# A two-layer streaming trunk on one core: norm matmuls, one branch tile, layer-B norms, value tiles and key weights reordered

## The chip, the core and the metric

The kernel runs on one core of a Trainium2 chip. The core has a matrix engine (TensorE, "PE"; its weight loads are listed as "PEld"), a vector engine (DVE), an activation engine (ACT), a general engine (POOL) and a queue engine (SP) which here only issues DMA transfers. ACT and POOL issue transfers too. Each engine works through its own stream in order; semaphores tie the streams together. Matmul results go to PSUM, which the kernel uses as eight banks of 128 x 512 float32, and ACT or DVE bring them to SBUF.

The metric is device time of one execution in microseconds, the median of several runs. Lower is better.

## The reference, cut to what matters

One inference step over 1024 prompt frames and 32 sample frames (1056 columns), model width 1024. Layer A is a gated linear recurrence, layer B is banded attention, and both read the residual stream through RMS norms:

```python
# layer A (width 1408, 16 blocks of 88 for the gates)
u = rmsnorm(x, norm_pre) @ w_in                 # branch | gate
conv = conv_b + sum(ext[:, tap:tap+T] * conv_w[tap] for tap in range(4))
r = sigmoid(conv_blocks @ w_r + b_r); i = sigmoid(conv_blocks @ w_i + b_i)
a = exp(-8 * r * softplus(-lam)); b = sqrt(1 - a*a) * (i * conv)
h = scan(a, b)                                  # h_t = a_t h_(t-1) + b_t
x1 = x + rmsnorm((h * silu(gate)) @ w_out, norm_post)
# shared keys and values
kv = rmsnorm(x1, norm_kv) @ w_kv;  k = rope(kv[:256]);  v = kv[256:]
# layer B: 16 query heads on 4 key heads, window 128, a sink per head
u = rmsnorm(x1, norm_pre_b) @ w_in_b;  q = rope(u[:1024])
y = x1 + rmsnorm((attend(q, k, v) * silu(u[1024:])) @ w_out_b, norm_post_b)
```

Outputs are `y` for all frames, the last convolution inputs and recurrence states, the keys and values of the last 128 prompt frames and those of the sample frames.

## The kernel before, in words

**Tiles.** Activations are held transposed: 128 channels on the partitions, frames along the free axis. The frames fall into three column blocks, n = 0, 1, 2, of 384, 384 and 292 columns in layer A (`NSA`; 292 with gaps) and 384, 384 and 288 in layer B (`NSB`). Weights come as 128 x 128 tiles.

**Three matmuls for one.** Each float32 operand is split into a high part (rounded) and a low part (the rest). A product is three matmuls: high by high, high by low, low by high (`mm3`, lines 150 to 152, and `mm3_steps`, line 698, which yields after every six matmuls so that others can be put between). The high part is made on ACT (line 116, or 120 with a gain), the low part on DVE (line 117 or 121), for a few weights on POOL.

**Weights.** `weights` loads a matrix in groups of four 128 x 128 tiles into a ring called `raw` (four buffers, shared by every weight of the kernel) and splits them into rings `whi` and `wlo` (six buffers each). A gain of a norm is folded in: for the names in `GAIN_ACT` in the split itself, for others by a product on POOL first (line 132).

**The order.** Each engine's stream is laid out when the kernel is built, by a planner which simulates the engines and takes, among the instructions that it thinks ready, the one that comes first in the program. `urgent()` moves an instruction ahead by 300 places. `pin()` ties an instruction behind the one which the program names before it on the same engine. At run time the streams are fixed: an engine whose next instruction isn't ready waits.

**The start of layer A.** The three first branch tiles are multiplied column block by column block (`first_mm`, with x not yet normed), because x arrives in blocks. `x_stat(n)` makes the row statistics and a diagonal matrix of the norm's scale; `x_norm(n)` spreads it over the partitions with one matmul per 128 frames (line 296, tile `rs`), then scales the open PSUM banks (line 207, DVE), and runs the convolution (line 222 on ACT, 224 on DVE) and the split of its result into `chi` and `clo`. `x_norm(0)` comes behind branch tile 1 of block 1, `x_norm(1)` behind branch tile 0 of block 2, `x_norm(2)` at the end.

**The loop over the other branch tiles** (line 445): step t multiplies branch tile t (t from 3), loads weights two tiles ahead, and runs the gate matmuls of tile t - 3 (`GATES_AT`). Gate blocks of 88 channels don't agree with tiles of 128, so a gate takes its own tile (three matmuls, lines 150 to 152, tile `gt`) and a few rows of the neighbours, which `pack_rows` copies by DMA into a tile `pack` (line 371, matmuls at 390 and 391). The first gates stand in step 3, behind branch tile 3.

**From layer A to layer B.** The w_out_a product runs block by block, eight output tiles each (`oa`). Beside it the norms run as generators: `norms_a(n)` has eleven steps, namely the residual loads (16 transfers for block 2), the post-norm's sum (`ss_p`, line 158) and factor, one step for each of eight tiles (scale on DVE, line 601; add the residual, 607; split into `xh`, `xl`; square), and at last the second norm's sum (`ss_x`) and factor `r1`, which scales the rope tables on POOL (636). `NORM_AT` says how many steps of which block's generator run behind each output tile, `NORM_KV` how many in each key block: its first entry inside `rope`, behind the key matmuls, its second behind the value rows.

**Keys and values.** For each column block: `k_block(n)` multiplies the two key halves (`rAk`, `rBk`, 24 matmuls each, line 698), runs `norm()`, rotates (715 to 717), splits and stores; then `v_rows(n)` makes two value tiles (`vc`, lines 150 to 152), scaled by `r1` (765). `v_blocks(n)` transposes them, 128 frames at a time (`v_block(t)`, two pinned transposes, line 775), and splits and stores the result. The blocks of n = 0 and 1 are transposed behind the next key block, all three at once; those of n = 2 behind the first query block, when PSUM has been divided anew and matmul tiles have three banks.

**Layer B** goes on with query blocks (`q_block`, the same `rope`), attention head group by head group with gate tiles and the next group's queries between, and the output product with its norm. The last 256 frames leave through `out_t`.

Of the kernel before, what the change touches and what calls it, by code (L numbers as in the profile page):

```python
# [9 lines left out]
F32 = mybir.dt.float32  # L10
# [7 lines left out]
P = 128  # L18
# [45 lines left out]
def _trunk(ctx, tc, nc, A):  # L64
# [58 lines left out]
    def weights(src, kn, name, gain=None):  # L123

        out = []
        for k0 in range(0, kn, 4):
            kk = min(4, kn - k0)
            raw = ring.tile([P, 4, P], F32, tag="raw", bufs=4, name=f"raw_{name}_{k0}")
            nc.sync.dma_start(raw[:, :kk, :], src[:, k0:k0 + kk, :])
            if gain is not None and name not in GAIN_ACT:  # L130
                with urgent():
                    G.tensor_tensor(raw[:, :kk, :], raw[:, :kk, :],
                                    gains[:, gain * KD + k0:gain * KD + k0 + kk].unsqueeze(2).to_broadcast([P, kk, P]),
                                    op=ALU.mult)
            hi = ring.tile([P, 4, P], F32R, tag="whi", bufs=6, name=f"whi_{name}_{k0}")
            lo = ring.tile([P, 4, P], F32R, tag="wlo", bufs=6, name=f"wlo_{name}_{k0}")
            with urgent():
                if name in GAIN_ACT:
                    for i in range(kk):
                        split_scaled(hi[:, i, :], lo[:, i, :], raw[:, i, :], g_of(gain, k0 + i))  # L140
                else:
                    split(hi[:, :kk, :], lo[:, :kk, :], raw[:, :kk, :], G if name in LO_POOL else None, name in HI_DVE)
            out += [(hi[:, i, :], lo[:, i, :]) for i in range(kk)]
        return out

    def mm3(ps, ws, xs, last=True):

        n = len(ws)
        for i, ((wh, wl), (xh, xl)) in enumerate(zip(ws, xs)):
            nc.tensor.matmul(ps, wh, xh, start=i == 0, stop=False)  # L150
            nc.tensor.matmul(ps, wh, xl, start=False, stop=False)  # L151
            nc.tensor.matmul(ps, wl, xh, start=False, stop=last and i == n - 1)  # L152

# [32 lines left out]
    def x_of(c0, c1):  # L186
        return [(xhi[k][:, c0:c1], xlo[k][:, c0:c1]) for k in range(KD)]

    conv, chl, ext, gw, pack = {}, {}, {}, {}, {}

    def branch_mm(t, ns=(0, 1, 2)):
        if t not in ext:
            ext[t] = row(f"ext{t}")
            G.memset(ext[t][:, 0:3], 0.0)
        banks = []
        for n in ns:
            c0, c1 = NSA[n]
            ps = bank(f"br{t}_{n}")
            mm3(ps[:, :c1 - c0], wts[t], x_of(c0, c1))
            banks.append((n, ps))  # L200
        return banks

    def branch_evac(t, banks):
        for n, ps in banks:
            c0, c1 = NSA[n]
            with urgent():
                V.tensor_tensor(ext[t][:, 3 + c0:3 + c1], ps[:, :c1 - c0], rs[:, c0:c1], op=ALU.mult)
# [83 lines left out]
    def x_norm(n):  # L291

        ps = bank(f"rs{n}")
        for i, t in enumerate(range(3 * n, 3 * n + 3)):
            m = P if t < 8 else DEC
            pin(nc.tensor.matmul(ps[:, i * P:i * P + m], ones[:m], diag[:m, t * P:t * P + m], start=True, stop=True))
        with urgent():
            if n < 2:
                S.activation(rs[:, NSA[n][0]:NSA[n][1]], ps[:, :384], AF.Copy, scale=1024.0)
            else:  # L300
                S.activation(rs[:, 768:SEQ], ps[:, :256], AF.Copy, scale=1024.0)
                S.activation(rs[:, S0:S0 + DEC], ps[:, 256:256 + DEC], AF.Copy, scale=1024.0)
        for m in range(NS):
            branch_evac(m, open_[n][m])
        for m in range(NS):
            branch_conv(m, n)

    open_ = {0: [], 1: [], 2: []}

    def first_mm(n, m):  # L310
        if n == 0 and m:
            prep_in(m)
        open_[n].append(branch_mm(m, (n,)))

    x_split(0)
    for m in range(NS):
# [10 lines left out]
    x_stat(1, xr[1])  # L327
    for n in (1, 2):
        for m in range(NS):
            first_mm(n, m)  # L330
            if m == 2 - n:
                x_norm(n - 1)
        if n == 1:
            x_stat(2, xr[2])
    x_norm(2)
# [108 lines left out]
    GATES_AT = ((), (), (), (0,), (1,), (2,), (3,), (4,), (5,), (6,), (7,), (8, 9, 10))  # L444
    for t in range(MR):
        if t >= NS:
            branch_evac(t, branch_mm(t))
        wts.pop(t)
        if t >= NS - 2:
            prep_in(t + 2)  # L450
        with urgent():
            if t >= NS:
                branch_conv(t)
            if t >= 1:
                prep_gate(t - 1)
        ri = [gates(i) for i in GATES_AT[t]]
        with urgent():
            if t >= NS:

                split(*chl[t], conv[t], behind=True)  # L460
            if t >= 1:
                pack_rows(t - 1)
        for i, g in zip(GATES_AT[t], ri):
            recur(i, g)
# [175 lines left out]
            next(na[int(i)], None)  # L640


    NORM_AT = ((), ("0", "00", "00", "00", "00", "", "", ""), ("1", "11", "110", "11", "11", "", "", ""))
    NORM_KV = (("1", "2" * 10), ("", ""), ("2", ""))
    korder = [k for k in range(MR) if k not in LATE] + list(LATE)
    REUSE = 2
    orders = [list(range(KD))]
# [85 lines left out]
    def k_block(n, wA, wB, norm):  # L733
        nm = f"k{n}"
        c0, c1 = NSB[n]
        run(rope(n, wA, wB, nm, norm))
        a, b = rope_out.pop(nm)
        q = halves(nm, a, b, c1 - c0)
        dst = kscr.rearrange("x p c -> p x c")
        if n < 2:  # L740
            nc.sync.dma_start(dst[:, :, c0:c1], q.bitcast(F32))
        else:
            nc.sync.dma_start(dst[:, :, c0:SEQ], q[:, :, :256].bitcast(F32))
            nc.sync.dma_start(dst[:, :, 1152:1184], q[:, :, 256:256 + DEC].bitcast(F32))
            for i, x in enumerate((a, b)):
                nc.sync.dma_start(A["o_k"][i], x[:, 128:256 + DEC])
# [10 lines left out]
    def v_rows(n):  # L757

        c0, c1 = NSB[n]
        out = []  # L760
        for i in range(2):
            ps = bank(f"vc{n}_{i}")[:, :c1 - c0]
            mm3(ps, wts[f"v{i}"], x1_of(c0, c1))
            u = unit(f"vc{n}_{i}", w=c1 - c0)
            V.tensor_tensor(u, ps, r1[:, c0:c1], op=ALU.mult)
            out.append(u)
        return out

    def v_block(t, rows_):
# [11 lines left out]
            nc.sync.dma_start(A["o_v"][(t - 7) * P:(t - 7) * P + m], f[:m, :256])  # L781

    vrows = {}

    def v_blocks(n):
        for t in range(3 * n, 3 * n + 3):
            v_block(t, vrows[n])

    def prep_v():

# [37 lines left out]
    prep_v()  # L828
    for n in range(3):
        k_block(n, wts["kA"], wts["kB"], lambda: pump(NORM_KV[n][0]))  # L830
        if n:
            v_blocks(n - 1)
        vrows[n] = v_rows(n)
        pump(NORM_KV[n][1])
    for nm in ("kA", "kB", "v0", "v1"):
# [138 lines left out]
    def finish_og(g, n):  # L974
# [6 lines left out]
                ogl[m, n] = t  # L981
        del TT[g, n]

    for nm, mi in (("qA0", 0), ("qB0", 1)):
        prep_m(nm, A["w_in_b"][mi], KD, 3)
    for n in range(3):
        run(q_block(0, n))
        if n == 0:
            v_blocks(2)

    def fillers(g):
        for m in (2 * g, 2 * g + 1):
# [253 lines left out]
```

## Time and profile before

| | |
|---|---|
| median of 3 runs | 905.42 us (905.33 to 906.95) |
| profiled execution | 905.81 us, span 904.0 us |
| PE busy | 885.4 us, 98% of the span, 5434 matmuls |
| DVE, ACT, POOL busy | 708.1, 563.1, 221.7 us |
| granted PE clock, mean | 0.995 |
| DMA | 137.35 MB, 152 GB/s |

A row of a timeline gives start, duration, engine, line, operation, output and inputs, and shape; in brackets the idle time ahead of it and what ended it. "x3" merges three such instructions. PE matmuls overlap, so that their durations (0.34 us for 384 columns) are about twice the distance of their starts; the distance is what counts for the time. A row of a stretch gives its bounds, its length, the busy time of each engine with the number of instructions, the granted PE clock as a share, the busy share of the DMA engines and GB/s. A row of the waits gives who waited for whom, the sum, how often, and the longest.

### The profile page before, as it was taken

To read this page: it belongs to the slowest core of one execution; us is meant where nothing else is said; L and a number is where in the kernel's file an instruction comes from. 1 tells how busy PE (TensorE), PEld (TensorE's weight loads), DVE (VectorE), ACT (ScalarE), POOL (GpSimd) and SP (SyncE) were. 2 spreads that over 40 slices of the span, in tenths; PEclk is the share of its full clock that TensorE was granted. 3 is DMA by queue.
4 is the path that set the end of the run, shared out by engine and by line. 5 is a ranking of instruction groups with operands and counts; after the bars stand their busy time and mean duration, and the time that the engine had idled before them with its cause. 6 is when DMAs were issued, how large, how long until landed. Compare 5 with 4: busy or idle time off the path is not lost. (4 is left out here: it accounts for less than half of the span.)

```text
span 904.0 us, 15787 instructions
## 1 busy us (share of the span) xinstructions
PE 885.4 (98%) x5434; PEld 864.4 (96%) x5434; DVE 708.1 (78%) x1499; ACT 563.1 (62%) x1231; POOL 221.7 (25%) x263
## 2 busy tenths in 40 slices
PE   9989999999999999999999999999999999999997
PEld 8989999999999999999989899999999999999975
DVE  6797878878897654177897847999999989998776
ACT  8748877879454325364663527766767757797661
POOL 5250212114300001126362432122122011202330
PEclk9999999999999999999999999999999999999999
DMA  9522433242533216445545667338338338334884
GB/s 337 204 75 77 135 88 125 81 128 92 181 119 124 89 57 190 146 135 178 163 157 186 210 205 205 98 111 231 96 110 239 103 97 239 121 112 160 281 250 144
DMA packets 95777, 137.35 MB, mean 152 GB/s; under 512 B 16144, under 2 KB 64304, under 8 KB 95696
## 3 DMA queue, kind: packets, MB, share of 16 engines
q1 hardware_dynamic: 86040, 123.30, 43.9%
q10 hardware_dynamic: 9480, 12.49, 4.5%
q8 instruction: 43, 0.70, 0.3%
q0 software_dynamic: 176, 0.54, 0.2%
q14 instruction: 38, 0.31, 0.1%
HBM read 99.28 MB, written 32.13 MB: 145 GB/s over the span
## 5 line engine op out<-in xcount | busy, mean ns | idle before, releaser
L150 PE MATMUL oa<-yh,whi_outa 128*128 128x384 f32 (+1 forms) x264 | 85.8, 326 | 0.0
L151 PE MATMUL gb<-xlo,whi_ina 128*128 128x384 f32 (+1 forms) x264 | 85.6, 324 | 0.0
L152 PE MATMUL gb<-xhi,wlo_ina 128*128 128x384 f32 (+1 forms) x264 | 85.4, 323 | 0.0
L150 PE MATMUL gb<-xhi,whi_ina 128*128 128x384 f32 (+1 forms) x264 | 85.2, 323 | 0.0
L151 PE MATMUL oa<-yl,whi_outa 128*128 128x384 f32 (+1 forms) x264 | 85.1, 323 | 0.0
L152 PE MATMUL oa<-yh,wlo_outa 128*128 128x384 f32 (+1 forms) x264 | 85.1, 323 | 0.0
L616 POOL TENSOR_TENSOR qp<-qp,qp 128x384 f32<-128x384 f32 (+2 forms) x34 | 49.3, 1449 | 138.2 <-ACT qp L614 126.5
L150 PE MATMUL br<-xhi,whi_ina 128*128 128x384 f32 (+1 forms) x240 | 77.8, 324 | 0.0
L151 PE MATMUL br<-xlo,whi_ina 128*128 128x384 f32 (+1 forms) x240 | 77.8, 324 | 0.0
L152 PE MATMUL br<-xhi,wlo_ina 128*128 128x384 f32 (+1 forms) x240 | 77.4, 323 | 0.0
L117 DVE TENSOR_TENSOR wlo_outa<-raw_outa,whi_outa 128x512 fp32r<-128x512 f32 (+1 forms) x60 | 43.7, 742 | 42.7 <-ACT whi_outa L116 42.6
L931 ACT ACTIVATE P<-P,sm 128x257 f32<-128x257 f32 (+1 forms) x132 | 64.3, 490 | 8.0 <-DVE sm L928 7.9
L698 PE MATMUL gB<-xl,whi_g 128*128 128x384 f32 (+1 forms) x192 | 63.0, 328 | 0.0
L698 PE MATMUL gB<-xh,whi_g 128*128 128x384 f32 (+1 forms) x192 | 62.9, 328 | 0.0
L698 PE MATMUL gB<-xh,wlo_g 128*128 128x384 f32 (+1 forms) x192 | 62.6, 326 | 0.0
L116 ACT ACTIVATE whi_outa<-raw_outa 128x512 fp32r<-128x512 f32 (+1 forms) x60 | 35.5, 594 | 41.5 <-PE oa L151 25.1
L224 DVE SCALAR_TENSOR_TENSOR conv<-ext,pa,conv 128x1060 f32<-128x1060 f32 (+2 forms) x51 | 50.2, 1005 | 9.0 <-ACT conv L222 8.6
L928 DVE CUSTOM_DVE_ANT_0 P<-S,mask,nsnk 128x256 f32<-128x256 f32 (+1 forms) x128 | 52.8, 463 | 4.9 <-PE S L926 4.8
L151 PEld LDWEIGHTS oa<-yl,whi_outa 128*128 128x128 f32 x264 | 49.6, 188 | 0.4
L150 PEld LDWEIGHTS oa<-yh,whi_outa 128*128 128x128 f32 x264 | 49.6, 188 | 0.4
L150 PEld LDWEIGHTS gb<-xhi,whi_ina 128*128 128x128 f32 x264 | 49.7, 188 | 0.0
L152 PEld LDWEIGHTS oa<-yh,wlo_outa 128*128 128x128 f32 x264 | 49.7, 188 | 0.0
(301 smaller groups left out, 2894.0 us busy)
## 6 DMA issues: line engine op xcount, KB each, us to landing
raw_ina<-w_in_a SPq DMA_DIRECT2D x44, 256.0 KB, 2.8
raw_outa<-w_out_a SPq DMA_DIRECT2D x40, 256.0 KB, 2.7
raw_ob<-w_out_b SPq DMA_DIRECT2D x32, 256.0 KB, 2.6
qscr<-quadq SPq DMA_DIRECT2D x8, 768.0 KB
Q<-qscr SPq DMA_DIRECT2D x32, 192.0 KB, 4.3
hscr<-u SPq DMA_DIRECT2D x11, 530.0 KB, 3.0
xr<-xr SPq DMA_DIRECT2D x8, 512.0 KB, 10.2
raw_g<-w_in_b SPq DMA_DIRECT2D x16, 256.0 KB, 3.3
```

What stands on the lines that cost most here:

```text
L116: pin(S.activation(dst_hi, src, AF.Copy), behind)
L117: (lo_eng or V).tensor_tensor(dst_lo, src, dst_hi.bitcast(F32), op=ALU.subtract)
L150: nc.tensor.matmul(ps, wh, xh, start=i == 0, stop=False)
L151: nc.tensor.matmul(ps, wh, xl, start=False, stop=False)
L152: nc.tensor.matmul(ps, wl, xh, start=False, stop=last and i == n - 1)
L224: V.scalar_tensor_tensor(c, e[:, c0 + k:c1 + k], pa[:, t, k:k + 1], c, op0=ALU.mult, op1=ALU.add)
L616: G.tensor_tensor(sums[0], sums[0], q, op=ALU.add)
L698: nc.tensor.matmul(ps, l, r, start=c == 0, stop=c == 3 * n - 1)
L928: V.tensor_tensor_reduce(pt[:, h, :w], sb[:, (h - h0) * 256:(h - h0) * 256 + w], msk, -0.125, nsnk[:, sk][:, h:h + 1], op0=ALU.add, op1=AL ...
L931: S.activation(pt[:, h, :w + 1], pt[:, h, :w + 1], AF.Exp, bias=nmax[:, h:h + 1], scale=-1.0, accum_out=rsum[:, h:h + 1])
```

## The change

There are seven edits:

1. `mm3` gets a callback `mid`, run in the middle of a product, and a flag `behind` which pins its first matmul. `x_norm(0)` now stands in the middle of branch tile 1 of block 1, and `x_norm(1)` in the middle of branch tile 0 of block 2, with the matmul that follows pinned; the next tile's first matmul is pinned too.
2. Column blocks 0 and 1 of branch tile 4 move into step 3, ahead of the first gates. Column block 2 stays in step 4.
3. The loads of the first key weights (kA) get two buffers of their own in the pool `late` instead of two of the four in the ring.
4. Norm steps: block 1 keeps its eighth tile step for key block 0, and its last step for the place behind the value rows of block 0. Block 2's residual loads and its post-norm's sum move into key block 0, behind the key matmuls; its eight tile steps follow behind the value rows, as before.
5. Value tiles of blocks 0 and 1 are transposed one by one: two inside the next key block (after 18 matmuls of each key half) and one between the two value products.
6. Those of block 2 are spread over the first two query blocks (`V_AT`): after 18 matmuls of the second half of query block 0, and after 18 of each half of query block 1.
7. POOL's gain products of qA1 and qB1 are pinned behind POOL's earlier work in the program.

```diff
+            if name == "kA":
+                raw = late.tile([P, 4, P], F32, tag="raw", bufs=2, name=f"raw_{name}_{k0}")
+            else:
+                raw = ring.tile([P, 4, P], F32, tag="raw", bufs=4, name=f"raw_{name}_{k0}")
...
+                    pin(G.tensor_tensor(raw[:, :kk, :], raw[:, :kk, :],
...
+                                        op=ALU.mult), name in ("qA1", "qB1"))
...
-    def mm3(ps, ws, xs, last=True):
+    def mm3(ps, ws, xs, last=True, mid=None, behind=False):
...
-            nc.tensor.matmul(ps, wh, xh, start=i == 0, stop=False)
+            if mid and i == n // 2:
+                mid()
+            pin(nc.tensor.matmul(ps, wh, xh, start=i == 0, stop=False), behind and i == 0 or mid and i == n // 2)
...
-            first_mm(n, m)
-            if m == 2 - n:
-                x_norm(n - 1)
+            first_mm(n, m, (lambda: x_norm(n - 1)) if m == 2 - n else None, m == 3 - n)
...
-            branch_evac(t, branch_mm(t))
+            branch_evac(t, branch_mm(t, (2,) if t == 4 else (0, 1, 2)))
...
+        if t == 3:
+            branch_evac(4, branch_mm(4, (0, 1)))
...
-    NORM_AT = ((), ("0", "00", "00", "00", "00", "", "", ""), ("1", "11", "110", "11", "11", "", "", ""))
-    NORM_KV = (("1", "2" * 10), ("", ""), ("2", ""))
+    NORM_AT = ((), ("0", "00", "00", "00", "00", "", "", ""), ("1", "11", "110", "1", "1", "1", "", ""))
+    NORM_KV = (("122", "1" + "2" * 8), ("", ""), ("2", ""))
...
-        run(rope(n, wA, wB, nm, norm))
+        for step, _ in enumerate(rope(n, wA, wB, nm, norm)):
+            if n and step in (2, 6):
+                v_block(3 * n - 3 + step // 4, vrows[n - 1])
...
+            if n and i == 0:
+                v_block(3 * n - 1, vrows[n - 1])
...
-        if n:
-            v_blocks(n - 1)
...
+    V_AT = {(0, 6): 6, (1, 2): 7, (1, 6): 8}
...
-        run(q_block(0, n))
-        if n == 0:
-            v_blocks(2)
+        for step, _ in enumerate(q_block(0, n)):
+            if (n, step) in V_AT:
+                v_block(V_AT[n, step], vrows[2])
```

More of the change, by code (lines that the diff above doesn't have):

```diff
@@ L127, in weights @@
             kk = min(4, kn - k0)
-            raw = ring.tile([P, 4, P], F32, tag="raw", bufs=4, name=f"raw_{name}_{k0}")
+            if name == "kA":
+                raw = late.tile([P, 4, P], F32, tag="raw", bufs=2, name=f"raw_{name}_{k0}")
+            else:
+                raw = ring.tile([P, 4, P], F32, tag="raw", bufs=4, name=f"raw_{name}_{k0}")
             nc.sync.dma_start(raw[:, :kk, :], src[:, k0:k0 + kk, :])
@@ L131, in weights @@
                 with urgent():
-                    G.tensor_tensor(raw[:, :kk, :], raw[:, :kk, :],
-                                    gains[:, gain * KD + k0:gain * KD + k0 + kk].unsqueeze(2).to_broadcast([P, kk, P]),
-                                    op=ALU.mult)
+                    pin(G.tensor_tensor(raw[:, :kk, :], raw[:, :kk, :],
+                                        gains[:, gain * KD + k0:gain * KD + k0 + kk].unsqueeze(2).to_broadcast([P, kk, P]),
+                                        op=ALU.mult), name in ("qA1", "qB1"))
             hi = ring.tile([P, 4, P], F32R, tag="whi", bufs=6, name=f"whi_{name}_{k0}")
@@ L189, in _trunk, with branch_mm @@
     conv, chl, ext, gw, pack = {}, {}, {}, {}, {}
-    def branch_mm(t, ns=(0, 1, 2)):
+    def branch_mm(t, ns=(0, 1, 2), mid=None, behind=False):
         if t not in ext:
@@ L198, in branch_mm @@
             ps = bank(f"br{t}_{n}")
-            mm3(ps[:, :c1 - c0], wts[t], x_of(c0, c1))
+            mm3(ps[:, :c1 - c0], wts[t], x_of(c0, c1), mid=mid, behind=behind)
             banks.append((n, ps))
@@ L308, in _trunk, with first_mm @@
     open_ = {0: [], 1: [], 2: []}
-    def first_mm(n, m):
+    def first_mm(n, m, mid=None, behind=False):
         if n == 0 and m:
             prep_in(m)
-        open_[n].append(branch_mm(m, (n,)))
+        open_[n].append(branch_mm(m, (n,), mid, behind))
     x_split(0)
@@ L783, in _trunk @@
     vrows = {}
-    def v_blocks(n):
-        for t in range(3 * n, 3 * n + 3):
-            v_block(t, vrows[n])
     def prep_v():
```

## The prediction

> **What bounds the kernel now.** I read the page, the waits by engine, the busy time of stretches, then the timelines around each hole in TensorE (PE).
>
> ```profile
> span 904.0 us, 15787 instructions
> PE 885.4 (98%) x5434; PEld 864.4 (96%) x5434; DVE 708.1 (78%) x1499; ACT 563.1 (62%) x1231; POOL 221.7 (25%) x263
> ...
> PE gt L150 <- ACT chi L116: 3.6, 1, 3.6
> PE rAk L698 <- DVE xl L117: 1.8, 2, 1.3
> PE rAk L698 <- DVE wlo_kA L121: 1.2, 3, 0.6
> PE v L775 <- DVE rp2q L715: 0.9, 1, 0.9
> ```
>
> PE bounds everything; the change adds and removes no PE work, so only its holes can be won. The four waits lie where the diff works. Their stretches (columns: PE, weight loads, DVE, ACT, POOL busy; granted clock; DMA):
>
> ```profile
> 58.40:62.20 3.80, 0.20 (x3) 0.01 (x1) 3.80 (x8) 1.55 (x4) 1.26 (x1) 0.93 0.02 8
> 62.20:65.50 3.30, 3.30 (x13) 3.30 (x14) 3.21 (x8) 1.28 (x3) 2.53 (x3) 0.56 0.53 148
> 465.60:472.50 6.90, 5.61 (x27) 4.03 (x26) 6.90 (x14) 4.03 (x14) 4.64 (x5) 1.00 0.15 54
> 472.50:504.00 31.50, 31.50 (x181) 30.96 (x180) 24.79 (x57) 14.72 (x40) 10.74 (x11) 1.00 0.63 196
> 504.00:509.80 5.80, 4.02 (x28) 3.55 (x27) 5.80 (x13) 2.07 (x6) 3.75 (x4) 1.00 0.29 108
> 520.50:532.00 11.50, 10.30 (x58) 9.45 (x58) 6.37 (x15) 2.37 (x7) 5.82 (x7) 1.00 0.57 168
> 874.70:877.10 2.40, 0.19 (x2) 0.13 (x2) 0.82 (x3) 2.25 (x5) 1.10 (x1) 1.00 0.93 304
> 877.50:880.90 3.40, 3.40 (x9) 2.49 (x8) 3.30 (x8) 1.27 (x4) 0.00 (x0) 0.50 0.83 228
> ```
>
> ```profile
> 57.38 0.33 PE L150 MATMUL gt<-chi,whi_gate 128*128 128x384 f32 x1
> ...
> 58.26 0.33 PE L152 MATMUL gt<-chi,wlo_gate 128*128 128x384 f32 x1
> 62.19 0.93 PE L150 MATMUL gt<-chi,whi_gate 128*128 128x292 f32 x2 [3.60 <-ACT chi L116]
> ...
> 65.47 0.34 PE L150 MATMUL br<-xhi,whi_ina 128*128 128x384 f32 x1
> ...
> 70.51 0.34 PE L152 MATMUL br<-xhi,wlo_ina 128*128 128x384 f32 x1
> 70.97 0.41 PE L390 MATMUL gt<-pack,whi_gate 96*128 96x384 f32 x1
> ...
> 504.23 0.29 PE L698 MATMUL rAk<-xh,whi_kA 128*128 128x288 f32 x1
> ...
> 506.63 0.29 PE L698 MATMUL rAk<-xh,whi_kA 128*128 128x288 f32 x1
> ```
>
> A 384-column matmul issues every 0.175 us (30 from 65.47 to 70.51), a 288-column one every 0.133 (19 from 504.23 to 506.63). So the gates lose 3.75 us waiting (58.26 + 0.175 to 62.19) and 0.44 x 3.3 = 1.45 to the halved clock, 0.2 more on either side: **5.4**. First key block: 6.9 - 27 x 0.175 = **2.2**. Last key block: 5.8 - 0.175 - 27 x 0.133 = **2.0**. Value tiles 6 to 8: 11.5 - 52 x 0.175 - 6 transposes at about 0.1 = **1.8**. Together 11.4, the most there is to win. (The hole at 874.7 lies in the output stage, which the diff leaves alone.)
>
> **The change part by part.** *Gates and tile 4.* 48 matmuls of tile 4 (8.4 us) now stand before the first gates, so gates start at 57.38 + 8.4 = 65.8, when chi and clo are there:
>
> ```profile
> 25.48 0.68 DVE L289 TENSOR_SCALAR diag<-ident,stat 128x128 f32<-128x128 f32 x3
> ...
> 31.73 1.49 DVE L207 TENSOR_TENSOR ext<-br,rs 128x384 f32<-128x384 f32 x3 [1.82 <-ACT rs L299]
> ...
> 34.74 0.67 DVE L289 TENSOR_SCALAR diag<-ident,stat 128x128 f32<-128x128 f32 x3
> ...
> 62.92 1.19 DVE L117 TENSOR_TENSOR clo<-conv,chi 128x292 fp32r<-128x292 f32 x3
> ...
> 63.07 2.74 ACTq L371 DMA_DIRECT2D pack<-chi  x3
> ...
> 63.39 2.83 SPq L371 DMA_DIRECT2D pack<-clo  x3
> ...
> DMA to landing us min/median/max: 6.5/6.5/6.5
> ...
> 29.64 0.38 PE L296 MATMUL rs<-diag,ones 128*128 128x128 f32 x2
> ...
> 37.70 0.38 PE L296 MATMUL rs<-diag,ones 128*128 128x128 f32 x2
> ```
>
> But what is late next is the packed rows: issued from 63.07 and 63.39, 6.5 us to landing, used at 70.97. Before, 30 matmuls of tile 4 filled that time; now they are spent, and after three native matmuls PE stands before a pack matmul at 65.8 + 0.5 = 66.3: 4.6 us early. The planner placed pack after 18 native and 30 tile-4 matmuls, that is at 57.4 + 2.9 + 5.3 = 65.6 had nothing waited, so it would see no reason to put the remaining 24 matmuls of tile 4 in between. Against this works the earlier norm: block 0's norm matmuls move from behind branch 1 to its middle, 12 x 0.175 = 2.1 us sooner (29.64 to 27.5), block 1's 12 x 0.133 = 1.6 sooner (37.70 to 36.1). The diagonals they read are there at 26.2 and 35.4, so these two pins cost PE nothing. DVE sat idle 1.82 us for rs and is full at 58 to 65 (3.80 of 3.80), so the chain to clo ends some 3 us sooner (2.1 plus scattered idle). Left-over wait 4.6 - 3 = 1.6, no halved clock: **-3.8**. Bounds: -5.4 (pack lands in time); +0.8 (nothing gained by DVE: 4.6 waited, 1.6 at half clock). Tile 4's evacuations, PSUM banks and its row only move; DVE has them to do anyway.
>
> *When the clock halves.* The waits for xl in key block 2 (1.3 us the longer) left the clock at 1.00; the one at 874.7 (2.4 us) was followed by 3.4 us at 0.50. I price a wait of over 2.4 us with 1.6 more. [...]
>
> *Keys and values.*
>
> ```profile
> 459.62 1.40 SPq L129 DMA_DIRECT2D raw_kA<-w_k  x2
> ...
> 490.52 8.41 SPq L580 DMA_DIRECT2D res<-xT  x16
> ...
> 465.68 5.74 DVE L121 SCALAR_TENSOR_TENSOR wlo_kA<-raw_kA,gains,whi_kA 128x128 fp32r<-128x128 f32 x8
> 471.34 2.18 DVE L121 SCALAR_TENSOR_TENSOR wlo_kB<-raw_kB,gains,whi_kB 128x128 fp32r<-128x128 f32 x8
> ...
> 489.94 1.01 DVE L765 TENSOR_TENSOR vc<-vc,r 128x384 f32<-128x384 f32 x2
> ...
> 498.79 0.84 DVE L607 TENSOR_TENSOR z<-z,res 128x288 f32<-128x288 f32 x1 [0.64 <-DMA res<-xT]
> ...
> 511.12 0.54 DVE L765 TENSOR_TENSOR vc<-vc,r 128x384 f32<-128x384 f32 x1
> ...
> 486.57 0.55 PE L698 MATMUL rAk<-xh,whi_kA 128*128 128x384 f32 x1
> ...
> 513.41 0.82 PE L775 MATMUL v<-ident,vc 128*128 128x128 f32 x6
> ```
>
> The kA loads no longer need a ring buffer that the last w_out_a tile holds until 459.6. The splits then wait only for the hi and lo rings (six each), free when the last but one tile has been used, some 4 us before kA at 465.7; kB takes the ring places. **-1.9**, bounds -2.2 and +1.0 (eight splits, 2.2 us by kB's row, pushing the last tile's own splits on a full DVE).
>
> The norm of block 2 starts a key block sooner: its 16 loads (8.41 us of SP issue, ahead of query and gate weights that are not used before 520) and its eight scale, add and split steps, which began at about 490, can begin near 478. That removes the wait for xl (2.0). In exchange block 1's last two norm steps move later. And the transposes, pinned in PE's order, come much sooner: tile 3's from 513.41 to 18 matmuls into key block 2, 504.23 + 2.4 = 506.6, or 504.7 with the 1.9 won. Their input, the second product of 511.12, was ready at 511.66: 7.0 us have to be caught up. DVE had 31.5 - 24.8 = 6.7 idle in 472.5 to 504 and 1.7 of key splits listed ahead that may come behind. I take 1.2 us of waiting there, and 0.4 at tile 0's (486.57 + 3.15 - 1.9 = 487.8, input at 490.95 behind a DVE idle stretch of 3.2). Sum **-0.4**; bounds -2.0, and +8.1 (below).
>
> Value tiles 6 to 8: spread, they no longer queue for three banks together, but query block 1 follows tile 6 by six matmuls (1.05 us), while a tile's copy and subtraction, 256 columns each, need by estimate two thirds of the 0.54 us at 511.12 each and the handing over, 1.0 to 1.3. **-0.7**; bounds -1.8 and +1.7 (wait for rope's release instead).
>
> Block 2's post-norm sum now stands behind kB of block 0, where PE is at 465.7 + 48 x 0.175 = 474.1. The squares that it sums come from ACT, which had 2.9 us free in 465.6 to 472.5 and so can have them done: **+0.3** for the last of them, bounds 0 and 1. The two pins on POOL's gain products change an order that the trace shows already: 0, covered by a POOL busy 25% (1.0 without).
>
> Sum: -3.8 - 1.9 - 0.4 - 0.7 + 0.3 = **-6.5**. The profiled execution took 905.81 (span 904.0 and 1.8 around it), so 899.3; it lies 0.4 over the median 905.42, so **898.9**.
>
> **The rivals.** *All holes close*: DVE keeps up and pack lands in time. For it: DVE idle 6.7. Against: full DVE at 58 to 65. 905.4 - 11.4 = 894.0.
> *The gate wait becomes a pack wait* of 3 us that halves the clock again: 4.6 of 5.4 stay; so the gates win 0.8 and the whole 3.5: 901.9. For it: 6.5 us to landing. Against: DVE's earlier start. [...]
> *The waits only move*: full pack wait (+0.8), nothing won in blocks 1 and 2 or tiles 6 to 8, only key weights: 905.4 + 0.8 - 1.9 + 0.3 = 904.6, no change.
> *Slower*: the pinned transposes of tile 3. If DVE catches up none of the 7.0 and has the deferred step too (three operations, 1.5), PE waits 8.5 and 1.6 at half clock, while the 2.0 is covered: +8.1. With -3.8 - 1.9 - 0.7 + 0.3: 907.4. It decides from a wait of 6.5 us (with 1.6 for the clock 8.1, what the rest wins: 6.1 and the covered 2.0), an input later than 511.2. Against it: a quarter of DVE's time was idle there.
>
> **How the numbers follow.** Forecast 0.46 (own range 896 to 901.5), all close 0.14, pack wait 0.18, only moved 0.13, slower 0.09. 0.2% (1.8 us) is about what can be told from no change. Faster 0.46 + 0.14 + 0.18 = 0.78, same 0.13, slower 0.09. Range 893.6 to 904.0: it leaves out most of the last two.
>
> **What would show it.** Right: 48 tile-4 matmuls from 57.4, gates from 65.8, the clock at 1.00 to 70, a PE wait for pack of 1 to 2 us; norm matmuls near 27.5 and 36; whi_kA before 463; no wait for wlo_kA; residual loads near 478; v transposes in six pairs. Wrong: a clock of 0.5 after 66; PE waiting at L775 for vc over 3 us; a new wait for wlo_outa before 465, or in stages the diff doesn't touch.

## The result, and the profile after

The changed kernel takes 900.56 us (median of 6 runs, 898.79 to 902.95) against 906.18 us for the kernel before beside it (6 runs, 904.64 to 908.52): ratio 0.9935, 95% interval 0.9917 to 0.9952, so 0.5 to 0.8% faster. 898.9 had been forecast, and the time lies inside the range. The profiled execution took 899.8 us. The head of its page:

```profile
span 898.0 us, 15789 instructions
PE 880.9 (98%) x5434; PEld 862.1 (96%) x5434; DVE 705.1 (79%) x1499; ACT 563.2 (63%) x1231; POOL 209.7 (23%) x263
```

PE issues the same 5434 matmuls in 6.0 us less span. The waits of PE (who waits for whom, sum, how often, longest):

```profile
PE v L784 <- DVE vc L772: 1.7, 2, 1.5
...
PE rAq L703 <- ACT vf L789: 1.4, 1, 1.4
...
PE rAk L703 <- DVE wlo_kA L121: 0.5, 1, 0.5
PE oa L157 <- DVE wlo_outa L117: 0.5, 1, 0.5
```

Those at the first loads, in the attention and in the output stage are left out here. Of the four waits of before that the prediction named, those for `chi` (3.6), `xl` (1.8) and rope's bank (0.9) are gone; the one for `wlo_kA` has shrunk from 1.2 to 0.5; and three new ones stand there: for a value product (1.5 at tile 0), for `vf` at tile 8 (1.4) and for `wlo_outa` (0.5).

Waits leave out the halved clock, and single executions scatter by up to 4.5 us around their median (905.87 against 901.42 with both layer A edits). So the kernels below are compared by **lost time per stage**: the distance between the starts of neighbouring matmuls less the usual distance for that shape (0.175 us for 384 columns, 0.133 for 288, and likewise for the others), summed over a stage of the profiled execution. The stages: *gates* (12 to 100 us), *last w_out_a* (from 420 us to the first key matmul), *keys to attention* (from there to the first scores).

| kernel | gates | last w_out_a | keys to attention | ratio to before (95%) |
|---|---|---|---|---|
| before | 5.88 | 0.40 | 7.97 | 1 |
| the change | 1.02 | 1.58 | 5.83 | 0.9935 (0.9917 to 0.9952) |
| norm edit alone | 2.49 | 0.46 | 8.80 | 0.9961 (0.9945 to 0.9976) |
| tile 4 alone | 4.40 | 0.44 | 9.41 | 0.9982 (0.9967 to 0.9998) |
| both layer A edits | 0.80 | 0.44 | 8.85 | 0.9964 (0.9945 to 0.9982) |
| the five others | 5.67 | 1.57 | 5.88 | 0.9993 (0.9981 to 1.0005) |
| change, kA in the ring | 0.82 | 1.58 | 8.57 | 0.9969 (0.9953 to 0.9986) |
| change, old norm steps | 0.77 | 0.46 | 7.71 | 0.9941 (0.9922 to 0.9959) |
| change, value tiles in threes | 0.77 | 1.57 | 10.46 | 0.9986 (0.9966 to 1.0005) |
| change, tiles 0 to 2 and 8 later | 0.78 | 1.58 | 4.89 | 0.9916 (0.9895 to 0.9937) |
| change, tile 8 later | 0.80 | 1.55 | 5.57 | 0.9923 (0.9901 to 0.9945) |
| the same, residual loads on POOL | 0.77 | 1.65 | 9.99 | 0.9968 (0.9955 to 0.9981) |
| tile 8 later, scales pinned | 0.77 | 0.65 | 12.34 | 1.0007 (0.9990 to 1.0025) |
| tiles 0 to 2, 8 later, scales pinned | 0.78 | 1.57 | 12.11 | 1.0004 (0.9987 to 1.0020) |

The other holes lie where no edit reaches, at the first loads (4.7 to 6.4 us over these kernels) and in the output stage (1.8 to 7.6). They are as large as the whole gain and differ from one execution to the next, which is why a single span settles nothing here. The stage figures scatter as well: the three kernels with layer A edits alone lose 0.8 to 1.4 us more between keys and attention than the kernel before, though none of their edits reaches there. So a difference of about 1 us in that column shows nothing by itself. Each ratio is to executions of the kernel before that were timed with that kernel, so kernels are compared by their ratios.

The gates of the changed kernel, first as stretches (PE, weight loads, DVE, ACT, POOL busy; granted clock; DMA), then as timeline rows, and at last the time from issue to landing, which the profile tells for one of the six copies into the packed rows:

```profile
58.82:67.21 8.39, 8.39 (x50) 8.39 (x49) 6.06 (x12) 4.92 (x7) 3.05 (x5) 1.00 0.57 156
67.21:75.00 7.79, 7.79 (x53) 7.79 (x53) 4.58 (x6) 5.11 (x9) 0.00 (x0) 1.00 0.07 17
```

```profile
59.94 1.20 DVE L117 TENSOR_TENSOR clo<-conv,chi 128x292 fp32r<-128x292 f32 x3
60.42 2.84 SPq L374 DMA_DIRECT2D pack<-clo  x3
...
28.62 0.83 PE L301 MATMUL rs<-diag,ones 128*128 128x128 f32 x6
...
67.21 0.34 PE L155 MATMUL gt<-chi,whi_gate 128*128 128x384 f32 x1
67.73 0.34 PE L393 MATMUL gt<-pack,whi_gate 96*128 96x384 f32 x1
...
DMA to landing us min/median/max: 4.5/4.5/4.5
```

PE is busy throughout and the clock stays at 1.00 (before: 0.56 in 62.2 to 65.5). `clo` is split at 59.94 instead of 62.92, 3.0 us sooner as forecast; the copies of `clo` into the packed rows are issued from 60.42 on instead of 63.39, and the one copy whose landing is told took 4.5 us instead of 6.5. If the last, issued near 62.2, takes as long, it is there by about 66.7 (an estimate), and the first matmul that reads them, at 67.73, follows without a wait. The norm matmuls stand at 28.62 (29.64 before, 27.5 forecast).

### The profile page after: what moved, and what is told of

It is laid out like the page before. It is cut to its first block, busy times and chain, and to the rows that moved or that the text cites. A ratio compares the mean times of both kernels' runs of the same rounds, so it can differ in the third digit from the quotient of the medians.

```text
span 898.0 us, 15789 instructions
## 1 busy us (share of the span) xinstructions
PE 880.9 (98%) x5434; PEld 862.1 (96%) x5434; DVE 705.1 (79%) x1499; ACT 563.2 (63%) x1231; POOL 209.7 (23%) x263
## 5 line engine op out<-in xcount | busy, mean ns | idle before, releaser
L621 POOL TENSOR_TENSOR qp<-qp,qp 128x384 f32<-128x384 f32 (+2 forms) x34 | 41.0, 1207 | 147.2 <-ACT qp L619 135.3
L229 DVE SCALAR_TENSOR_TENSOR conv<-ext,pa,conv 128x1060 f32<-128x1060 f32 (+2 forms) x51 | 46.2, 925 | 10.7 <-ACT conv L227 10.2
```

The costliest lines, as they stand in the source:

```text
L229: V.scalar_tensor_tensor(c, e[:, c0 + k:c1 + k], pa[:, t, k:k + 1], c, op0=ALU.mult, op1=ALU.add)
L621: G.tensor_tensor(sums[0], sums[0], q, op=ALU.add)
```

## The experiments

### Layer A: the norm edit and tile 4, alone and together

The norm edit alone (edit 1; `mm3`'s callback and flag, and):

```diff
-            first_mm(n, m)
-            if m == 2 - n:
-                x_norm(n - 1)
+            first_mm(n, m, (lambda: x_norm(n - 1)) if m == 2 - n else None, m == 3 - n)
```

> The kernel before with edit 1 alone (norm matmuls in the middle of a branch tile). Theory A (the DVE chain to chi and clo is what the gates wait for, and the earlier norm shortens it by some 4 us, as clo at 59.9 instead of 62.9 in the changed kernel with a start 1.1 us later shows): the wait of 3.75 us at the first gates shrinks to under 1 us, the clock stays at 1.00, about 4.5 to 5.4 us faster. Theory B (tile 4's 48 matmuls are what covers the wait; the norm only moves DVE work): the wait stays above 2.5 us and the clock still halves, under 1.5 us faster.

Tile 4 alone (edit 2):

```diff
-            branch_evac(t, branch_mm(t))
+            branch_evac(t, branch_mm(t, (2,) if t == 4 else (0, 1, 2)))
...
+        if t == 3:
+            branch_evac(4, branch_mm(4, (0, 1)))
```

> The kernel before with edit 2 alone (column blocks 0 and 1 of branch tile 4 ahead of the first gates). Theory A: chi and clo as late as before, pack issued from 63 and landing 6.5 us later, gates at 65.8: PE waits 3 to 4.6 us at the first pack matmul and the clock halves, within 1 us of before. Theory B: pack's transfers land sooner when PE's order is another (4.5 us to landing in the changed kernel), so the wait is 1 to 2.5 us without a halved clock: 3 to 4.5 us faster.

Both, and nothing else:

> The kernel before with edits 1 and 2, nothing of layer B. Both theories: no wait at the gates, 5.4 us faster in that stage; if the parts add up, the stages from 455 on look as before and the whole is about 5.4 us faster, nearly all of the 5.6 to 6 us measured for the whole change.

Measured: 901.59, 903.54 and 901.42 us; lost time at the gates 2.49, 4.40 and 0.80 of the 5.88 before. One row of the norm edit alone, then of tile 4 alone its wait and two stretches:

```profile
64.54 0.45 PE L390 MATMUL gt<-pack,whi_gate 96*128 96x384 f32 x1 [1.04 <-DMA pack<-clo]
```

```profile
PE gt L390 <- DMA pack<-clo: 2.2, 1, 2.2
```

```profile
66.68:69.25 2.57, 0.34 (x3) 0.06 (x2) 1.37 (x2) 2.42 (x2) 0.00 (x0) 1.00 0.70 188
...
70.00:73.20 3.20, 3.20 (x14) 3.20 (x13) 2.22 (x3) 1.54 (x3) 0.00 (x0) 0.52 0.01 2
```

Tile 4 alone does what the rival "the gate wait becomes a pack wait" said: the wait for `chi` goes, one of 2.2 us for the packed rows comes, and the clock halves behind it (0.52 in 70.00 to 73.20). It wins 1.5. The norm edit alone takes the chain to `clo` forward and wins 3.4, though 1.0 of pack wait stays. Together they win 5.1, about the sum of the two (4.9): each covers what the other leaves.

The whole times say less than the gates: by the ratios the three kernels are 3.5, 1.6 and 3.3 us faster than before. Both edits together can't be told from the norm edit alone, and the 5.4 us expected of both lie outside their interval (1.6 to 5.0); 0.9 us of what is missing was lost between keys and attention, within the scatter named above. The norm edit alone fell short of its theory A, 4.5 to 5.4, which had not named the pack wait of 1.04 that stayed. Of tile 4 neither theory held whole: the rows landed sooner, as theory B said, and the clock halved all the same, as theory A said.

### Layer B's edits without layer A's

The change without edits 1 and 2.

> The changed kernel with edits 1 and 2 undone, so only the layer B edits (3 to 7). If the parts add up: gates wait 3.6 us as before with the halved clock, and 0.5 to 2 us faster in all (holes of the key and value stages 6.0 us before, 4.6 to 5 after: 0.8 won on the first key weights, 2.0 on the last key block, 1.5 given back at value tile 0 and 1.4 kept at value tile 8). A rival: the layer B edits are worth 3 us or more and the layer A edits less than 3.

903.99 us, ratio 0.9993: not to be told from no change. In lost time the edits win 2.1 between keys and attention and give 1.2 back at the last w_out_a tiles, 0.9 together. Added to the new layer A they win 1.9 (8.85 + 0.44 against 5.83 + 1.58); the two ratios, 0.9964 and 0.9935, have intervals that overlap, so that no interplay of the halves is shown.

### Key weights in the ring

The change without edit 3: the kA loads share the ring again.

```diff
-            if name == "kA":
-                raw = late.tile([P, 4, P], F32, tag="raw", bufs=2, name=f"raw_{name}_{k0}")
-            else:
-                raw = ring.tile([P, 4, P], F32, tag="raw", bufs=4, name=f"raw_{name}_{k0}")
+            raw = ring.tile([P, 4, P], F32, tag="raw", bufs=4, name=f"raw_{name}_{k0}")
```

> The changed kernel with edit 3 undone: kA's raw weights in the ring again. My prediction's step (their own buffers win 1.9 us): the hole at the first key block grows from about 1.4 us (0.7 before wlo_kA, 0.7 before the last wlo_outa) to 2.2 or more, 0.8 to 1.9 us slower than the changed kernel. Rival (the hi and lo rings and a full DVE set the time, not the raw buffers): the hole stays at 1.4 us, within 0.3 us of the changed kernel.

902.71 us; lost time between keys and attention 8.57 against 5.83. But not where it was expected. Rows of this kernel (its line numbers stand 3 lower):

```profile
454.73 3.20 SPq L129 DMA_DIRECT2D raw_kA<-w_k  x2
...
464.83 4.95 SPq L796 DMA_DIRECT2D raw_v<-wv  x4
...
463.51 0.44 PE L700 MATMUL rAk<-xh,wlo_kA 128*128 128x384 f32 x1 [0.54 <-DVE wlo_kA L121]
...
475.66 0.45 PE L152 MATMUL vc<-xh,wh_v 128*128 128x384 f32 x1 [0.73 <-ACT wh_v L120]
489.27 0.33 PE L781 MATMUL v<-ident,vc 128*128 128x128 f32 x1 [2.04 <-DVE vc L769]
```

and the answering rows of the changed kernel:

```profile
459.43 9.11 SPq L799 DMA_DIRECT2D raw_v<-wv  x4
...
463.92 0.45 PE L703 MATMUL rAk<-xh,wlo_kA 128*128 128x384 f32 x1 [0.54 <-DVE wlo_kA L121]
```

The wait in the first key block is 0.54 in both. With the other edits in place kA is loaded at 454.73 through the ring itself (before: 459.62). What the buffers of their own move is the queue behind kA: SP issues the value weights from 459.43 instead of 464.83, and without that the first value product waits (0.73), tile 0's transposes wait 2.04 instead of 1.46, and a halved clock follows: from 490.15 to 491.75 the matmuls with 384 columns start 0.32 us apart instead of 0.175, and the next key half loses 1.66. A halved clock behind tile 0 also comes in the kernel with tile 8 alone (0.56, below), which has the buffers, so how much of the 2.7 us belongs to the queue, and how much to the clock, isn't shown.

### Old norm steps

The change without edit 4 (the old entries of `NORM_AT` and `NORM_KV`).

> The changed kernel with edit 4 undone: norm steps where they were, value tiles still one by one. The prediction's slower case (transposes pinned before their input is ready) should show here in full: residual loads again near 490, PE waits at the transposes of value tile 3 for vc by 3 us or more and for xl in key block 2, clock possibly halved; 2 to 8 us slower than the changed kernel. Rival (DVE has room enough): waits for vc under 2 us in all, at most 1.5 us slower.

898.62 us, ratio 0.9941: no difference from the change that can be told. The 2 to 8 us expected did not come; the rival, that DVE has room enough, held. Its key weights (ACT, DVE, then PE), and the wait at the transposes:

```profile
457.81 1.28 ACT L120 ACTIVATE whi_kA<-raw_kA,gains 128x128 fp32r<-128x128 f32 x4
...
460.68 4.90 DVE L121 SCALAR_TENSOR_TENSOR wlo_kA<-raw_kA,gains,whi_kA 128x128 fp32r<-128x128 f32 x8
...
461.81 0.44 PE L703 MATMUL rAk<-xh,wlo_kA 128*128 128x384 f32 x1 [1.38 <-DVE wlo_kA L121]
```

```profile
PE v L784 <- DVE vc L772: 1.2, 1, 1.2
```

With kA's own buffers and the old norm steps the first key block loses 2.85 us, as much as before the change (2.62): the splits begin at 460.68, 0.8 us behind PE, although ACT had made its first four halves from 457.81 on. So it is edit 4, not edit 3, that shrinks this hole, to 0.80 (PE's waits for `wlo_kA` sum to 1.2 to 1.7 us in the five kernels without edit 4 and to 0.5 to 0.8 in the nine with it), and in part it only moves it a step ahead, to where block 1's deferred steps meet the last splits of w_out_a. These are the rows of the changed kernel:

```profile
458.53 0.87 DVE L117 TENSOR_TENSOR wlo_outa<-raw_outa,whi_outa 128x512 fp32r<-128x512 f32 x1 [1.54 <-ACT whi_outa L116]
459.32 1.16 DVE L612 TENSOR_TENSOR z<-z,res 128x384 f32<-128x384 f32 x1
460.40 1.37 DVE L117 TENSOR_TENSOR wlo_outa<-raw_outa,whi_outa 128x384 fp32r<-128x384 f32 x1
...
461.82 0.40 PE L157 MATMUL oa<-yh,wlo_outa 128*128 128x288 f32 x1 [0.52 <-DVE wlo_outa L117]
```

The last w_out_a tiles and the first key block together lose 3.0 before the change, 3.3 here, 2.4 in the changed kernel and 2.4 with kA in the ring. Over all stages edit 4 is worth 0.8 us of lost time (0.46 + 7.71 against 1.58 + 5.83), which is within the scatter. And the wait at tile 3's transposes stays at 1.2 us even without the earlier norm of block 2: the "slower" rival needed 6.5.

### Value tiles in threes

The change without edits 5 and 6.

```diff
-            if n and step in (2, 6):
-                v_block(3 * n - 3 + step // 4, vrows[n - 1])
...
+        if n:
+            v_blocks(n - 1)
```

> The changed kernel with edits 5 and 6 undone: value tiles transposed in threes, as before. Theory: one by one costs more than it brings, since the waits for vc (1.5 us at tile 0, 0.4 at tile 3) and for vf at tile 8 (1.4) go and the wait for rope's release at tiles 7 and 8 (0.9 to 1.3) and the wait at the first query block (0.3 to 0.8) come back: 0.5 to 2 us faster than the changed kernel. Rival: the threes then hold back PE at key block 2, since their splits come at once: 0 to 2 us slower.

903.01 us, ratio 0.9986, and 10.46 us lost: the expectation had the sign wrong. Rows of this kernel's ACT, DVE and PE, then the stretch behind:

```profile
512.77 0.38 ACT L116 ACTIVATE v<-v 128x256 fp32r<-128x256 f32 x1 [5.75 <-DMA vscr<-v]
...
513.18 0.42 DVE L117 TENSOR_TENSOR v<-v,v 128x256 fp32r<-128x256 f32 x1 [4.41 <-ACT v L116]
...
516.18 0.81 DVE L770 TENSOR_TENSOR vc<-vc,r 128x288 f32<-128x288 f32 x2
...
516.69 0.69 PE L703 MATMUL rAq<-xh,whi_qA 128*128 128x384 f32 x1 [3.72 <-DVE vc L770]
```

```profile
516.69:522.00 5.31, 5.31 (x17) 5.31 (x18) 1.29 (x3) 0.64 (x2) 0.52 (x1) 0.50 0.55 170
```

Two buffers hold the split value tiles until they are stored. Three tiles in a row make the third wait for the first one's store (ACT 5.75 us); DVE stands behind ACT with the rope and value products queued after it, PE behind DVE for a bank, and the clock stands at 0.50 for the 5.31 us of the stretch. One tile at a time keeps a store between each two. Before the change ACT waited for that store too, but PE got on, because its next bank was freed by the third tile's split and not by the value product behind it; these are the rows of before:

```profile
520.00 0.39 ACT L116 ACTIVATE v<-v 128x256 fp32r<-128x256 f32 x1 [4.08 <-DMA vscr<-v]
...
520.90 0.44 PE L698 MATMUL rAq<-xh,whi_qA 128*128 128x384 f32 x1 [0.27 <-DVE v L117]
```

Why the bank is another one in this kernel was not tried, so how much of the 4.6 us belongs to the store and how much to the bank stays open.

### Which of the waits that stay can still go

Tile 8 was given a later place, in query block 2, and tiles 0 to 2 one place later each:

```diff
-    V_AT = {(0, 6): 6, (1, 2): 7, (1, 6): 8}
+    V_AT = {(0, 6): 6, (1, 2): 7, (2, 2): 8}
...
-            if n and step in (2, 6):
-                v_block(3 * n - 3 + step // 4, vrows[n - 1])
+            if n and step in ((2, 6) if n == 2 else (6,)):
+                v_block(3 * n - 3 + (step // 4 if n == 2 else 0), vrows[n - 1])
...
-            if n and i == 0:
-                v_block(3 * n - 1, vrows[n - 1])
+            if n and (i == 0 or n == 1):
+                v_block(3 * n - 1 - (n == 1 and i == 0), vrows[n - 1])
```

> The changed kernel with value tiles 0 to 2 one place later each (tile 0 after 18 matmuls of the second key half, tiles 1 and 2 behind the two value products) and tile 8 in query block 2 (after 18 matmuls of its first half) instead of query block 1. Theory: the wait for vc at tile 0 (1.5 us) and the one for vf behind tile 8 (1.4 us) go, nothing takes their place: holes from 455 to 545 us about 2.5 to 3 us smaller, 2 to 3 us faster than the changed kernel, 7 to 9 faster than before. Rival: a wait of DVE or of PSUM takes their place, under 1 us faster.

And tile 8 alone (the first of these three pieces):

> The changed kernel with value tile 8 transposed in query block 2 instead of query block 1; tile 0 stays where the change put it. The theory that the two last waits are separate, each set by where its own tile stands: the wait for vf of 1.4 us at tile 8 goes, the wait for the value product vc at tile 0 (1.5 to 2 us) stays, holes from the first key block to the attention 4.4 us (5.8 in the changed kernel, 4.9 with tile 0 later too), 899 us, 1.4 us under the changed kernel. The rival that tile 8's transposes collide with the copies of the next queries wherever they stand: a wait of over 1 us near 540, no gain.

896.63 us (ratio 0.9916), the lowest of all here, and 897.99 (0.9923); the intervals overlap each other and the change's. The wait for `vf` is gone in both. Tile 0's wait stays in both, and moving it wins nothing: 1.8 us are lost at its new place too, and 1.1 at the new place of tile 3. That the second kernel lost 5.57 instead of the 4.4 expected is the clock. Stretches of the kernel with tile 8 alone, of the change, and of the kernel with both moves, each from the last matmul before the wait at tile 0, and the 3 us that follow:

```profile
484.67:486.84 2.17, 0.34 (x2) 0.02 (x1) 2.17 (x8) 2.17 (x7) 1.25 (x1) 1.00 0.83 284
...
487.60:490.80 3.20, 3.20 (x13) 3.20 (x13) 3.20 (x6) 2.56 (x8) 3.04 (x4) 0.56 0.83 303
```

```profile
486.12:487.91 1.79, 0.33 (x3) 0.01 (x2) 1.79 (x7) 1.79 (x6) 0.70 (x1) 1.00 0.80 271
...
488.60:491.80 3.20, 3.20 (x20) 3.17 (x20) 3.20 (x6) 2.15 (x7) 3.04 (x4) 1.00 0.85 309
```

```profile
488.16:490.11 1.95, 0.34 (x3) 0.02 (x2) 1.95 (x4) 1.93 (x6) 1.79 (x3) 1.00 0.78 284
...
491.00:494.00 3.00, 3.00 (x19) 3.00 (x18) 3.00 (x5) 1.01 (x3) 2.84 (x4) 1.00 0.39 136
```

PE stood idle for 1.8 us with tile 8 alone (the length less PE's busy time), for 1.5 in the change and for 1.6 with both moves. Only behind the 1.8 did it run at 0.56 for the next 3.2 us, which lost 1.6 more: about what the move was expected to win.

Why is tile 0's product late? These are the changed kernel's rows on SP, ACT, DVE and PE:

```profile
475.25 5.69 SPq L585 DMA_DIRECT2D res<-xT  x10
480.99 0.43 SPq L132 DMA_DIRECT2D raw_qA<-w_in_b  x1
...
483.91 0.40 ACT L120 ACTIVATE whi_qA<-raw_qA,gains 128x128 fp32r<-128x128 f32 x1 [4.36 <-DMA raw_qA<-w_in_b]
...
487.31 0.54 DVE L772 TENSOR_TENSOR vc<-vc,r 128x384 f32<-128x384 f32 x1
...
487.91 0.33 PE L784 MATMUL v<-ident,vc 128*128 128x128 f32 x1 [1.46 <-DVE vc L772]
```

Two causes offer themselves: the query weights, whose second load stands behind block 2's residual loads on SP and holds ACT for 4.36 us, and DVE's own queue, which has block 2's scales and additions ahead of the product. The first was taken away by issuing the 16 residual loads from POOL:

```diff
-            nc.sync.dma_start(dst[:, o:o + c1 - c0], src[:, c0:c1])
+            eng.dma_start(dst[:, o:o + c1 - c0], src[:, c0:c1])
...
-            load_parts(res, src[m], parts)
+            load_parts(res, src[m], parts, nc.gpsimd if (gain, n) == (1, 2) else nc.sync)
```

> The same, with block 2's 16 residual loads issued by POOL instead of SP. The theory that tile 0's product is late because the second load of raw_qA stands behind those loads on SP (at 480.99 and 483 on ACT in the changed kernel): raw_qA's load is issued 5 us or more earlier, ACT's wait of 4.4 us for it goes, tile 0's transposes wait under 0.5 us, holes from the first key block to the attention under 3.2 us, 897.5 us. The rival that DVE's own amount of work between the two key blocks sets the product's time: the wait at tile 0 stays over 1.2 us, 899 us as with tile 8 alone.

901.95 us, 9.99 lost. SP, DVE and PE of this kernel:

```profile
468.55 1.12 SPq L132 DMA_DIRECT2D raw_qA<-w_in_b  x2
...
481.42 3.04 DVE L606 TENSOR_TENSOR z<-z,r 128x288 f32<-128x288 f32 x8
...
491.25 0.55 DVE L772 TENSOR_TENSOR vc<-vc,r 128x384 f32<-128x384 f32 x1
...
491.85 0.33 PE L784 MATMUL v<-ident,vc 128*128 128x128 f32 x1 [2.69 <-DVE vc L772]
```

The second load came 12 us sooner than in the change, ACT's wait at 483 was gone, and the products came no sooner: DVE now took all eight scales, five additions and two rope products ahead of the first (487.52) and more ahead of the second. The value products, too, waited 1.5 us for weights that were now split behind the query weights. So the late load isn't the cause by itself. But this run changed more than the load: DVE stood idle 3.10 us for the first query weights (until 474.52), and POOL made its second sum for rope at 488.46 instead of 481.51, behind two products for the gate weights. The second cause was then taken away by pinning the scales at their place in the program, behind the value products, with tiles 0 to 2 at the change's place and at the later one:

```diff
-                pin(V.tensor_tensor(zs[m], zs[m], r, op=ALU.mult), gain == 4 or n < 2)
+                pin(V.tensor_tensor(zs[m], zs[m], r, op=ALU.mult))
```

> Value tile 8 in query block 2, and block 2's eight scale steps on DVE pinned at their place in the program, that is behind the two value products of block 0 (before, DVE took all eight scales and six residual additions ahead of the first product). The theory that DVE's own order makes tile 0 late: the products are done near 479 and 483, tile 0's transposes near 485 wait under 0.4 us, 1.5 to 2.0 us of holes go, no wait for xl appears in key block 2 since the last split is done near 496 and used after 504, holes from the first key block to the attention 3.6 us, 896.3 us. The rival that ACT's late half of raw_qA (5 us of waiting at 483) holds quadk and through it DVE: the second product stays behind 488, a wait of over 1 us stays, 898 us.

> The same with value tiles 0 to 2 one place later, as in the kernel with both moves. By the theory that DVE's order is the cause nothing is left to win by moving them: holes and time as with the pin alone, 896.3 us within 1. By the rival the later place takes what the pin leaves: 1 us less than with the pin alone.

905.57 and 905.04 us: all of the gain gone. DVE, ACT and PE of the first of the two:

```profile
483.75 0.65 DVE L121 SCALAR_TENSOR_TENSOR wlo_qA<-raw_qA,gains,whi_qA 128x128 fp32r<-128x128 f32 x2 [4.22 <-ACT whi_qA L120]
484.31 0.55 DVE L772 TENSOR_TENSOR vc<-vc,r 128x384 f32<-128x384 f32 x1
...
506.40 0.44 ACT L116 ACTIVATE xh<-z 128x288 fp32r<-128x288 f32 x1 [1.48 <-DVE z L612]
...
506.90 0.61 PE L703 MATMUL rAk<-xh,whi_kA 128*128 128x288 f32 x1 [1.28 <-ACT xh L116]
```

With none of block 2's tile steps ahead of it, DVE stands idle 4.22 us for the late query weights, and the first product comes at 484.31, sooner than in the change (487.31) but not at 479; tile 0's transposes still wait 0.6 and 1.1 us. The eight norm steps then run in lockstep, scale, addition, ACT's split, DVE's split, 2.3 us each, and the last `xh` is made at 506.40, when key block 2 already wants it: PE waits 1.28 us twice, and 1.87 for tile 3's product.

So the rows speak for both causes, one behind the other: with the pin the late query weights hold DVE, with the early load the scales and additions do, and in the change DVE's scales fill the time in which the query weights are not there. Their shares aren't shown, since each of these edits also laid other work in another order, and both together (the loads from POOL and the pin) weren't tried.

## Why the prediction was right, and where its steps were not

The time was right because most of the gain was put at the gates, 3.8 of 6.5 us, and came from there. That the sum came so close is in part luck: the gates won 1.1 us more than forecast, the other terms about 1.0 instead of 2.7, and the two misses nearly cancel. By steps, in lost time of the two profiled executions:

| step | forecast | measured |
|---|---|---|
| gates and tile 4 | -3.8 | -4.9 (5.88 to 1.02) |
| key weights | -1.9 | -0.6: first key block 2.62 to 0.80, last w_out_a tiles 0.40 to 1.58 |
| block 2's norm, pinned transposes | -0.4 | -0.3: key block 2 2.31 to 0.35, tile 0 0.20 to 1.86 |
| value tiles 6 to 8 | -0.7 | +0.1 (1.44 to 1.58) |
| block 2's sum, POOL's pins | +0.3 | about 0: +0.2 ahead of the second key half, -0.3 in the value products |

**Gates and tile 4**: right in mechanism, one term mis-sized. `clo` came 3.0 us sooner, as worked out, and gates started at 67.21 (65.8 forecast). The pack wait of 1.6 that was left over didn't come. The later start alone leaves 0.2 of it (rows at 70.9 - 3.0 = 67.9, the first pack matmul at 67.73), and the copy that landed in 4.5 us instead of 6.5 covers that. With tile 4 alone the copy took 4.2, and the wait was 2.2 where the same working without DVE's gain gave 4.6. Why that copy was faster with a layer A edit (4.8 us with the norm edit, 4.2 with both) was not tried; it stays open.

**Key weights**: the step that failed, in reason and in size. "The kA loads no longer need a ring buffer" is not what shrinks the wait for `wlo_kA`: with the ring it is the same 0.54, and with own buffers and the old norm steps it is back at 1.38. DVE was late with the splits because it was full of norm steps, and edit 4 thins these out; a part of the wait came back for `wlo_outa`, as named under "wrong", and from edit 4, not from kA's splits. Edit 3 earns its 2.7 us of lost time elsewhere; what the rows show there is that it moves the value weights 5.4 us ahead on SP. The working had costed the load that is moved, and not the queue behind it.

**Block 2's norm and the transposes**: the sum was right by luck, its parts exchanged. The wait of 1.2 was put at tile 3 and 0.4 at tile 0; tile 3's is 0.2 and tile 0's 1.5. DVE did catch up the 7 us, so the "slower" rival is out; what was missed is that the 16 residual loads, correctly costed as 8.41 us of SP ahead of the query weights, delay weights that ACT and DVE have in their order much sooner than "not used before 520". Nor was the earlier norm needed to end the wait for `xl`: with the old norm steps nobody waits for `xl` either, only 1.22 us for the product at tile 3, and not at all at tile 0. Edit 4 takes the one wait away and brings the other. Which edit ended the wait for `xl` was not tried.

**Value tiles**: -0.7 at tiles 6 to 8 didn't come; the wait moved to `vf` at tile 8 and went only when tile 8 did. But to undo both tile edits costs 4.6 us of lost time: three tiles in a row wait for the store of the first, which no step named.

**Clock**: a wait of over 2.4 us was priced with 1.6 more. The price is right (1.6 in the kernel with tile 8 alone), the condition was not. The 2.4 was the length of the stretch from 874.7; PE's own wait in it was 2.2. These are idle times of PE, and the clock behind them:

| kernel | PE idle, until | clock behind |
|---|---|---|
| the change | 1.36 us, 534.85 | 1.00 in 534.85 to 538.50 |
| the change | 1.46, 487.91 | 1.00 in 488.60 to 491.80 |
| change, tiles 0 to 2 and 8 later | 1.6, 490.11 | 1.00 in 491.00 to 494.00 |
| change, tile 8 later | 1.83, 486.84 | 0.56 in 487.60 to 490.80 |
| before | 2.2, 876.97 | 0.50 in 877.49 to 880.90 |
| tile 4 alone | 2.23, 69.25 | 0.52 in 70.00 to 73.20 |
| change, value tiles in threes | 3.72, 516.69 | 0.50 in 516.69 to 522.00 |
| tile 8 later, scales pinned | 1.28 twice, 504.59 and 506.90 | 0.50 in 507.80 to 511.00 |

Here the half clock followed waits of 1.83, 2.2 and 2.23 us, all under 2.4, and two waits of 1.28 us that ended 2.3 us apart, while a single one of 1.6 left the clock at 1.00. So the length of a single wait doesn't settle it. What does isn't shown.

**Signs**: of those named under "wrong", a new wait for `wlo_outa` before 465 came (0.52 at 461.82). Of those named under "right", the wait for `wlo_kA` stayed at 0.54, no wait for pack came, and tile 0's two transposes stand apart, at 487.91 and 491.20.

## What to carry to other kernels

Before a wait for a weight is put down to the buffer it is loaded into, see what the engine that splits it is doing: here buffers of its own left that wait as it was, and what they moved was the transfers queued behind. When an instruction is late behind two things in a row, taking one away can show the other instead of a gain; look at both queues before choosing. And the length of a wait of PE alone doesn't give its price: read the clock in the stretch behind it too. Here 1.83 us with tile 8 alone were followed by 3.2 us at 0.56, about 1.6 us more, and 1.6 us with both moves by 3 us at 1.00; two waits that differ by 0.2 us differed by about 1.8 in what they cost.

## What the runs showed of the hardware

- Before, the clock stood at 0.50 from 61.70 (0.5 us ahead of the end of PE's wait of 3.6 us) to 65.11, and from 877.49 (0.5 us behind the end of one of 2.2) to 880.90; it stood at 1.00 just ahead of both stretches and just behind them. With kA in the ring the matmuls with 384 columns started 0.32 us apart from 490.15 to 491.75, behind a wait of 2.04 us, instead of 0.175.
- Single waits of 1.36, 1.46 and 1.6 us left the clock at 1.00; waits of 1.83 us and more in the table above had 0.50 to 0.56 behind them, and so had two of 1.28 us close together. What sets this isn't shown.
- One of six small copies between SBUF tiles took 6.5 us from issue to landing before, and 4.8, 4.2, 4.2 and 4.5 with the norm edit, with tile 4, with both and in the change, though less DMA traffic lay around the slow one (167 GB/s over the copy before, 224 in the change).
- Residual loads cost the issuing queue 0.53 to 0.57 us each (ten in 5.69 us of SP in the change, sixteen in 8.41 before, fourteen in 7.43 us of POOL where POOL issues them), and in the change a weight load behind them on SP waits that out (480.99 behind 475.25 + 5.69).
